# Emptying masked score products by chunk in a chunked linear-attention stage

## The chip, the cores and the metric

One core of a Trainium2 chip runs the whole program. The metric is the device time of one execution in microseconds (us). The engines have a queue each and run side by side: TensorE (PE, matmuls; PEld is its weight loads), VectorE (DVE), ScalarE (ACT), GpSimd (POOL) and SyncE (SP, which issues most transfers). A matmul writes into one of eight banks of PSUM (128 partitions x 2 KB), and DVE or ACT must empty a bank before it is written again.

## The reference

One layer of a hybrid block over 2048 tokens of width 1024, in float32. A combined projection feeds a band attention, an RWKV-7 time mixing and two gates; the two results are projected, gated, added and normalised, and a squared-relu MLP follows. The change is in the time mixing:

```python
def step(state, inp):
    r_t, w_t, k_t, v_t, aa_t, bb_t = inp
    sa = jnp.einsum('bhij,bhj->bhi', state, aa_t)
    state = (state * w_t[:, :, None, :] + sa[..., None] * bb_t[:, :, None, :]
             + v_t[..., None] * k_t[:, :, None, :])
    y = jnp.einsum('bhij,bhj->bhi', state, r_t)
    return state, y
xs = tuple(jnp.moveaxis(t, 1, 0) for t in (r_h, w_h, k_h, v_h, -kk, kk * a_h))
_, ys = lax.scan(step, init, xs)
```

## The kernel before

The tokens are worked in four groups of 512 (`G`). For each group the program runs `phase_rwkv`, then attention, then the merge; the MLP follows in two halves. Matrix products in float32 are made of three products of high and low parts; the dense products (`psd`, L92 and L131, 24 matmuls of 128x512 for each 128 columns) read weights that ACT casts to the high part (`whi`, L81) and DVE splits into the low part (`wlo`, L83), both in two buffers.

The time mixing turns the scan over tokens into products over chunks of 64 tokens (`C`), 8 chunks a group (`NC`). Its 8 heads are worked in four pairs (`p` 0 to 3): one head in partitions 0 to 63, the other (`par`=1) in 64 to 127. For a pair, `rwkv_pre` makes r, k, v and the decay, and from these A (the scaled -kk), r (scaled) and the keys B and K. `AR` holds A and r, `BK` holds B and K. The scores `ps_A` are, for each chunk and head, one product of BK with AR (64 rows, 128x128): B and K against A and r of the same chunk. They fill one bank for four chunks of one head, so a pair has four banks in two halves (`h`) of two. They come from the pool `pa`, which has two banks and serves nearly everything in this stage; the pool `pr` has two more (`wus`), for the chunk chain `ps_st` and, later, `ps_yt`.

From the scores DVE takes, bank by bank: the part that the inverse needs, scaled by the reciprocal norm `n2` (`NA`, L596, two operations of 32 partitions); A's own scores under a strict mask (`mS`) into the other half of AR (L602); r's scores under an inclusive mask, times the norm, into `BR` (L603). POOL has multiplied mask and norm ahead of that (`mN`, L500). `rwkv_inverse` then inverts the 32x32 diagonal blocks of two pairs at once on DVE: a stream transpose of NA into N, 31 steps (T, X), and transposes back (X1, XD). `rwkv_blocks` joins the blocks by two rounds of small products (`ps_t`), and `rwkv_trans` turns A (`ps_at`, L680), makes `ps_w`, `ps_ug`, `ps_tq`, `ps_s` and `ps_y`, and `recurrence` walks the eight chunks: `ps_st` on TensorE, then ST on DVE (L743), chunk after chunk.

The instructions of all engines are put in order by a scheduler with its own estimate of times. A few TensorE instructions are held back behind a numbered dense matmul of the group (`place`): the first score of p=0 behind number 150 (`SCORES`), ps_t behind 412 and 424, and 640 and 653 (`BLOCKS`), A's turning in p=0 behind 438 (`TURNED`). `k` of p=3 and others are scaled out of a dense bank by ACT at L401, and `lora_g` is a cast of ACT (L81).

Of the kernel before, what the change touches and what calls it, by code (L numbers as in the profile page):

```python
# [18 lines left out]
P = 128  # L19
# [37 lines left out]
class Block:  # L57
# [100 lines left out]
    def constants(self, ctx, mixing):  # L158
# [36 lines left out]
        self.mS = cp.tile([P, C], F32, name="mS")  # L195
        self.mI = cp.tile([P, C], F32, name="mI")
        for t, op in ((self.mS, ALU.is_gt), (self.mI, ALU.is_ge)):
# [247 lines left out]
    def rwkv_pre(self, g, p, rp, NA, between=lambda: None):  # L445
# [52 lines left out]
        mN = self.tp.tile([P, 2, NC, C], F32, tag="mN", bufs=1, name="mN")  # L498
        for par in range(2):
            nc.gpsimd.tensor_tensor(  # L500
                mN[:, par],
                self.mI[:, None, :].to_broadcast((P, NC, C)),
                n2[:, :, par, None].to_broadcast((P, NC, C)),
                ALU.mult,
            )
        between()

        AR = rp.tile([P, NC, 3, C], F32, tag="AR", name="AR")
# [3 lines left out]
        for par in range(2):  # L512
            rw = slice(par * C, par * C + C)
            nc.vector.scalar_tensor_tensor(
                AR[rw, :, par], k3[rw], self.nkk[rw, col], E[rw, :, 0:C], op0=ALU.mult, op1=ALU.mult
            )
        nc.vector.tensor_tensor(AR[:, :, 2], r3, E[:, :, 1 : C + 1], ALU.mult)
# [42 lines left out]
        BR = rp.tile([P, NC, 2, 2, C], F32, tag="BR", name="BR")  # L560
# [15 lines left out]
        mS = self.mS[:, None, :].to_broadcast((P, 4, C))  # L576
        for h in range(2):
            cs = slice(h * 4, h * 4 + 4)

            both = [self.pa.tile([P, 4, P], F32, tag="a", name="ps_A") for _ in range(2)]  # L580
            for j in range(4):
                c = h * 4 + j
                for par, psA in enumerate(both):
                    rw = slice(par * C, par * C + C)
                    mm = nc.tensor.matmul(
                        psA[:, j].rearrange("p (s t) -> p s t", t=C),
                        BK[rw, c].rearrange("p s t -> p (s t)"),
                        AR[rw, c, par : 3 : 2 - par], start=True, stop=True,
                    )
                    if p == c == par == 0:  # L590
                        self.place(mm, SCORES)
            for par, psA in enumerate(both):
                ow = slice(C - par * C, P - par * C)
                for lo, w in ((0, C), (32, 32)):
                    hw = slice(par * C + lo, par * C + lo + 32)
                    nc.vector.tensor_tensor(  # L596
                        NA[hw, q, cs, 0:w],
                        psA[hw, :, lo : lo + w],
                        n2[hw, cs, par, None].to_broadcast((32, 4, w)),
                        ALU.mult,  # L600
                    )
                nc.vector.tensor_tensor(AR[ow, cs, par], psA[ow, :, 0:C], mS[ow], ALU.mult)  # L602
                nc.vector.tensor_tensor(BR[:, cs, par, 1], psA[:, :, C:P], mN[:, par, cs], ALU.mult)  # L603
# [3 lines left out]
    def rwkv_inverse(self, NA, rp):  # L607
# [4 lines left out]
            N, NA.rearrange("p q c t -> p t (q c)")[:, 0:32, None, :].to_broadcast((P, 32, 2, 2 * NC))  # L612
# [16 lines left out]
        X1 = ip.tile([P, 2, NC, 32], F32, tag="X1", name="X1")  # L629
# [12 lines left out]
    def rwkv_blocks(self, NA, Rs, b):  # L642

        nc, X1, XT = self.nc, self.X1, self.XT
        first, second = [], []
        Z = self.ip.tile([P, 2, NC, 32], F32, tag="Z", name="Z")
        parts = [(slice(r, r + 32), slice(r + 32, r + C)) for r in (0, C)]
        ps = self.pa.tile([P, 2, NC, 32], F32, tag="a", name="ps_t1")
        for q in range(2):
            for c in range(NC):  # L650
                for lo, hi in parts:
                    mm = nc.tensor.matmul(ps[hi, q, c], NA[lo, q, c, 32:64], X1[lo, q, c], start=True, stop=True)
                    first.append(mm)
        for lo, hi in parts:
            nc.scalar.copy(Z[hi], ps[hi])
        ps = self.pa.tile([P, 2, NC, 32], F32, tag="a", name="ps_t2")
        for q in range(2):
            for c in range(NC):
                for lo, hi in parts:
                    mm = nc.tensor.matmul(ps[lo, q, c], Z[hi, q, c], XT[hi, q, c, 32:64], start=True, stop=True)  # L660
                    second.append(mm)
        for mm, n in zip((first[0], second[0]), BLOCKS[b]):
            self.place(mm, n)
        for lo, hi in parts:
            nc.scalar.copy(XT[lo, :, :, 32:64], ps[lo])
        for q in range(2):
            Rs[q]["XT"] = XT[:, q]

    def rwkv_trans(self, p, R):
# [7 lines left out]
        for h, cs in enumerate(halves):  # L677
            ps = self.pa.tile([P, 4, P], F32, tag="a", name="ps_at")
            for j in range(4):
                mm = nc.tensor.transpose(ps[:, j], AR[:, h * 4 + j, 0:2].rearrange("p s t -> p (s t)"), self.ident)  # L680
                if p == 0 and h == 1 and j == 0:
                    self.place(mm, TURNED)
            for par in range(2):
                nc.scalar.copy(WA[rows[par], cs, 0], ps[rows[par], :, par * C : par * C + C])
        ps = self.pa.tile([P, NC, C], F32, tag="a", name="ps_w")
        for c in range(NC):
            for par in range(2):
                ow = rows[1 - par]
                nc.tensor.matmul(ps[rows[par], c], AR[ow, c, par], SV[ow, c, par], start=True, stop=True)
# [15 lines left out]
        for h, cs in enumerate(halves):  # L705
            ps = self.pa.tile([P, 4, 2, C], F32, tag="a", name="ps_tq")
            for j in range(4):
                c = h * 4 + j
                for par in range(2):
                    nc.tensor.matmul(  # L710
                        ps[rows[par], j], GT[rows[par], c], BR[rows[par], c, par], start=True, stop=True
                    )
# [3 lines left out]
            nc.vector.tensor_tensor(TQ[:, cs, 1], ps[:, :, 1], AR[:, cs, 2], ALU.add)  # L716
# [76 lines left out]
    def phase_rwkv(self, g, quads):  # L793
        tc = self.tc
        with ExitStack() as ctx:
# [13 lines left out]
            def pairs():  # L809
                return self.ip.tile([P, 2, NC, C], F32, tag="NA", name="NA")  # L810
# [20 lines left out]
            def rec_of(NA, Rs, b):  # L831
                self.rwkv_blocks(NA, Rs, b)
# [22 lines left out]
            rec = rec_of(NA, Rs, 0)  # L855
# [17 lines left out]
            for i in range(3):  # L873
                advance(inv, 8)
                gate()
                if i == 0:
                    b = rp.tile([P, 4, G], F32, tag="BR", name="cmb")
                    load([b[:, i] for i in range(4)])
                elif i == 1:
                    b, c = (rp.tile([P, n, G], F32, tag=t, name="cmb") for t, n in (("AR", 3), ("SV", 2)))  # L880
                    load([b[:, 0], b[:, 1], b[:, 2], c[:, 0]])
# [4 lines left out]
            rec = rec_of(NA, nxt, 1)  # L886
# [763 lines left out]
```

## Time and profile before

| | |
|---|---|
| median of 3 runs | 3199.93 us (3196.32 to 3201.05) |
| the profiled execution | 3198.07 us, span 3196.4 us |
| TensorE | 3147.3 us busy (98%) |
| DVE / ACT / POOL | 2235.8 / 1578.7 / 613.8 us busy |
| granted TensorE clock | 0.999 |

In the order of time each row has its start, its length, the engine and line, what it writes and reads, and the number of instructions that were merged; a bracket has the idle time ahead of it and who ended it. A matmul's length runs past the start of the next, so its price is the distance from start to start. A float32 matmul that is not a transpose leaves two records, so a score product of four chunks reads x8. In a list of waits each row has the total, how often, and the longest. Line numbers are those of the kernel before.

### The profile page before, as it was taken

Reading aid. Unit: us, or ns where it says so; the run is one execution under the profiler, and the core shown is the slowest. Engines: PE = TensorE matmul, PEld = TensorE weight load, DVE = VectorE, ACT = ScalarE, POOL = GpSimd, SP = SyncE. Lnnn points to the kernel's source line nnn. Section 1 sums busy time; section 2 is a strip of 40 time slices with the busy share of each in tenths; the row PEclk is TensorE's granted clock in tenths of the full one; section 3 lists DMA queues with packets and bytes.
Section 4 is the critical chain, followed back from the end, with each engine's and each line's share of the span. In section 5 each row is a group of like instructions: output and inputs, shape, how many; then the busy total and the mean of one; then the engine's idle time right before and its main releaser. Section 6 shows DMA issues by size and latency. Waiting matters only on the chain. (4 is left out here: it accounts for less than half of the span.)

```text
span 3196.4 us, 49803 instructions
## 1 busy us (share of the span) xinstructions
PE 3147.3 (98%) x18800; PEld 2575.3 (81%) x18800; DVE 2235.8 (70%) x3668; ACT 1578.7 (49%) x2511; POOL 613.8 (19%) x1119
## 2 busy tenths in 40 slices
PE   8999999999999999999999999999999999999998
PEld 6877788778888877888877888888888878888887
DVE  6785667776767786767876776877656768765564
ACT  5435645445745445745534755454544454444343
POOL 3222012132112222112222101221211112210000
PEclk9999999999999999999999999999999999999999
DMA  6245473157573246574236466554877866547565
GB/s 192 86 135 189 134 259 129 60 172 244 175 260 129 77 141 245 186 235 160 94 116 228 160 208 261 192 179 162 293 268 251 281 225 213 170 156 244 191 221 174
DMA packets 197477, 598.82 MB, mean 187 GB/s; under 512 B 25570, under 2 KB 25708, under 8 KB 197236
## 3 DMA queue, kind: packets, MB, share of 16 engines
q1 hardware_dynamic: 139124, 415.24, 40.1%
q0 software_dynamic: 48896, 163.61, 13.6%
q10 hardware_dynamic: 9216, 16.78, 1.4%
q8 instruction: 148, 2.42, 0.3%
q14 instruction: 93, 0.76, 0.1%
HBM read 431.67 MB, written 167.01 MB: 187 GB/s over the span
## 5 line engine op out<-in xcount | busy, mean ns | idle before, releaser
L1469 PE MATMUL ps_dn<-fop 128*128 128x512 f32 x2688 | 610.8, 389 | 0.0
L1469 PEld LDWEIGHTS ps_dn<-fop 128*128 128x128 f32 x2688 | 504.1, 188 | 104.7 <-DVE fop L83 0.2
L81 ACT CAST whi<-wraw 128x1024 fp32r<-128x1024 f32 x232 | 243.5, 1049 | 284.4 <-PE psd L92 202.5
L83 DVE TENSOR_TENSOR wlo<-wraw,whi 128x1024 fp32r<-128x1024 f32 x230 | 280.6, 1220 | 125.4 <-ACT whi L81 80.2
L92 PE MATMUL psd<-hh,whi 128*128 128x512 f32 x1328 | 357.9, 398 | 1.1 <-ACT k L401 1.0
L92 PE MATMUL psd<-hh,wlo 128*128 128x512 f32 x1328 | 356.8, 398 | 0.0
L92 PE MATMUL psd<-hl,whi 128*128 128x512 f32 x1328 | 354.3, 397 | 0.0
L92 PEld LDWEIGHTS psd<-hl,whi 128*128 128x128 f32 x1328 | 243.6, 188 | 47.9
L92 PEld LDWEIGHTS psd<-hh,wlo 128*128 128x128 f32 x1328 | 242.7, 188 | 48.3
L92 PEld LDWEIGHTS psd<-hh,whi 128*128 128x128 f32 x1328 | 241.2, 188 | 50.0 <-ACT k L401 1.6
L83 DVE TENSOR_TENSOR fop<-xraw,fop 128x1024 fp32r<-128x1024 f32 x112 | 137.0, 1223 | 176.2 <-ACT fop L81 175.8
L81 ACT CAST fop<-xraw 128x1024 fp32r<-128x1024 f32 x112 | 117.8, 1052 | 251.0 <-PE ps_dn L1469 191.9
L1339 POOL DMA_DIRECT2D xd<-X x192 | 104.1, 542 | 380.3 <-ACT X L1336 318.2
L83 DVE TENSOR_TENSOR fop<-wdraw,fop 128x1024 fp32r<-128x1024 f32 x112 | 136.6, 1219 | 19.7 <-ACT fop L81 19.4
L81 ACT CAST fop<-wdraw 128x1024 fp32r<-128x1024 f32 x112 | 117.6, 1050 | 35.7 <-DMA wdraw<-in_w_down_dram 22.7
L994 DVE CUSTOM_DVE_ANT_0 sc<-bias,ps_s 128x640 f32<-128x640 f32 (+4 forms) x128 | 93.8, 733 | 39.3 <-PE ps_s L988 23.3
L1012 DVE TENSOR_TENSOR PTl<-ps_pt,PTh 128x640 fp32r<-128x640 f32 (+4 forms) x128 | 94.3, 737 | 27.7 <-ACT PTh L1011 26.8
L1001 ACT ACTIVATE sc<-sc,mn 128x640 f32<-128x640 f32 (+4 forms) x128 | 97.8, 764 | 31.8 <-DVE mn L994 30.4
L81 ACT CAST s12h<-s 128x1024 fp32r<-128x1024 f32 x32 | 33.7, 1053 | 155.5 <-PE ps_u L92 155.5
L92 PE MATMUL ps_p<-yh,whi 128*128 128x512 f32 x256 | 101.7, 400 | 4.9 <-DVE th L1149 2.2
L92 PE MATMUL ps_p<-yl,whi 128*128 128x512 f32 x256 | 101.5, 397 | 0.3 <-DVE yl L83 0.2
L1178 PE MATMUL ps_o<-whi,mh 128*128 128x512 f32 x256 | 100.5, 392 | 0.7 <-DVE o L1189 0.6
(374 smaller groups left out, 6804.0 us busy)
## 6 DMA issues: line engine op xcount, KB each, us to landing
wraw<-in_w_in_dram SPq DMA_DIRECT2D x168, 512.0 KB, 3.7
xraw<-xd SPq DMA_DIRECT2D x112, 512.0 KB, 4.5
xd<-X POOLq DMA_DIRECT2D x192, 256.0 KB, 4.7
wraw<-in_w_up_dram SPq DMA_DIRECT2D x80, 512.0 KB, 4.4
wdraw<-wd SPq DMA_DIRECT2D x64, 512.0 KB, 4.8
wdraw<-in_w_down_dram SPq DMA_DIRECT2D x48, 512.0 KB, 5.0
gd<-gate ACTq DMA_DIRECT2D x64, 256.0 KB, 2.5
wd<-cmb POOLq DMA_DIRECT2D x64, 256.0 KB, 3.7
```

The costliest lines, as they stand in the source:

```text
L81: high = self.high = self.nc.scalar.copy(hi, src)
L83: self.low = lower.tensor_tensor(lo, src, hi.bitcast(F32), ALU.subtract).ins
L92: mm.append(nc.tensor.matmul(ps, l, r, start=n == 0, stop=n == last).ins)
L994: least = nc.vector.tensor_tensor_reduce(sc[:, 0:n], bias[:, s0:640], pss[:, c0 : c0 + n], 1.0, 3.0e38, ALU.add, ALU.min, mn,)
L1001: nc.scalar.activation(sc[:, 0:n], sc[:, 0:n], AF.Exp, scale=-1.0, bias=mn, accum_out=sm[:, col : col + 1])
L1012: nc.vector.tensor_tensor(lv, pst[:, 0:nk], hv.bitcast(F32), ALU.subtract)
L1178: nc.tensor.matmul(ps[t], l[:, k, ts], r[:, k % 2], start=k == 0 and j == 0, stop=k == KB - 1 and j == 2)
L1339: nc.gpsimd.dma_start(self.xd[q][i // 2][:, i % 2], src)
L1469: nc.tensor.matmul(ps, o[:, l, k, sl], o[:, r, k], start=start and n == 0, stop=stop and n == end)
```

## The change

- The two masks become one tile, inclusive and strict side by side, and POOL's product of mask and norm goes.
- `AR` has A and r in two planes. A is written by one DVE operation for both heads.
- Every chunk and head of the scores is emptied by one DVE operation (128 x 128: score times norm times mask) into BR, which has a third plane for A's scores; ACT copies from there the part that the inverse needs, 32 partitions at a time.
- `ps_t` and `ps_w` read BR's third plane. NA has half the width.
- `ps_at` turns A of two chunks in one transpose, so four transposes of one tile serve a pair instead of eight of two; four ACT copies take them to WA.
- In the first two pairs the second half of the scores uses the two banks of `pr`.
- The tiles that later hold loads for the MLP (`cmb`) are cut out of BR and AR differently.

```diff
-        mN = self.tp.tile([P, 2, NC, C], F32, tag="mN", bufs=1, name="mN")
-        for par in range(2):
-            nc.gpsimd.tensor_tensor(
-                mN[:, par],
-                self.mI[:, None, :].to_broadcast((P, NC, C)),
-                n2[:, :, par, None].to_broadcast((P, NC, C)),
-                ALU.mult,
-            )
...
-        AR = rp.tile([P, NC, 3, C], F32, tag="AR", name="AR")
+        AR = rp.tile([P, 2, NC, C], F32, tag="AR", name="AR")
...
-        for par in range(2):
-            rw = slice(par * C, par * C + C)
-            nc.vector.scalar_tensor_tensor(
-                AR[rw, :, par], k3[rw], self.nkk[rw, col], E[rw, :, 0:C], op0=ALU.mult, op1=ALU.mult
-            )
-        nc.vector.tensor_tensor(AR[:, :, 2], r3, E[:, :, 1 : C + 1], ALU.mult)
+        nc.vector.scalar_tensor_tensor(AR[:, 1], k3, self.nkk[:, col], E[:, :, 0:C], op0=ALU.mult, op1=ALU.mult)
+        nc.vector.tensor_tensor(AR[:, 0], r3, E[:, :, 1 : C + 1], ALU.mult)
...
-        BR = rp.tile([P, NC, 2, 2, C], F32, tag="BR", name="BR")
+        BR = rp.tile([P, NC, 2, 3, C], F32, tag="BR", name="BR")
...
-            both = [self.pa.tile([P, 4, P], F32, tag="a", name="ps_A") for _ in range(2)]
+            pool, tag = (self.pr, "wus") if p < 2 and h else (self.pa, "a")
+            both = [pool.tile([P, 4, P], F32, tag=tag, name="ps_A") for _ in range(2)]
...
             for par, psA in enumerate(both):
-                ow = slice(C - par * C, P - par * C)
-                for lo, w in ((0, C), (32, 32)):
-                    hw = slice(par * C + lo, par * C + lo + 32)
-                    nc.vector.tensor_tensor(
-                        NA[hw, q, cs, 0:w],
-                        psA[hw, :, lo : lo + w],
-                        n2[hw, cs, par, None].to_broadcast((32, 4, w)),
-                        ALU.mult,
-                    )
-                nc.vector.tensor_tensor(AR[ow, cs, par], psA[ow, :, 0:C], mS[ow], ALU.mult)
-                nc.vector.tensor_tensor(BR[:, cs, par, 1], psA[:, :, C:P], mN[:, par, cs], ALU.mult)
+                for j in range(4):
+                    c = h * 4 + j
+                    nc.vector.scalar_tensor_tensor(
+                        BR[:, c, par, 1:3].rearrange("p s t -> p (s t)"), psA[:, j], n2[:, c, par : par + 1], masks,
+                        op0=ALU.mult, op1=ALU.mult,
+                    )
+                for i in range(2):
+                    hw = slice(par * C + 32 * i, par * C + 32 * i + 32)
+                    cs = slice(h * 4, h * 4 + 4)
+                    nc.scalar.copy(NA[hw, q, cs], BR[hw, cs, par, 2, 32 * i : 32 * i + 32])
...
-        for h, cs in enumerate(halves):
-            ps = self.pa.tile([P, 4, P], F32, tag="a", name="ps_at")
-            for j in range(4):
-                mm = nc.tensor.transpose(ps[:, j], AR[:, h * 4 + j, 0:2].rearrange("p s t -> p (s t)"), self.ident)
-                if p == 0 and h == 1 and j == 0:
-                    self.place(mm, TURNED)
-            for par in range(2):
-                nc.scalar.copy(WA[rows[par], cs, 0], ps[rows[par], :, par * C : par * C + C])
+        ps = self.pa.tile([P, 4, P], F32, tag="a", name="ps_at")
+        for j in range(4):
+            mm = nc.tensor.transpose(ps[:, j], AR[:, 1, 2 * j : 2 * j + 2].rearrange("p c t -> p (c t)"), self.ident)
+            if p == j == 0:
+                self.place(mm, TURNED)
+        for par in range(2):
+            for h in range(2):
+                nc.scalar.copy(WA[rows[par], h:NC:2, 0], ps[rows[h], :, par * C : par * C + C])
```

With this the scheduler orders the stage anew; the order of the attention, the merge, the MLP and of SP's transfers stays. The names in the rows below are those of the words above; x8 of ps_A is eight products of which both heads alternate, unless said otherwise, x4 is four of one head.

TensorE in the first pair, before:

```order
L92 MATMUL psd<-hh,whi 128x512 x7
L585 MATMUL ps_A<-AR,BK 128x128 x8
L92 MATMUL psd<-hh,whi 128x512
L92 MATMUL psd<-hl,whi 128x512 x6
L585 MATMUL ps_A<-AR,BK 128x128 x4
L92 MATMUL psd<-hl,whi 128x512 x2
L585 MATMUL ps_A<-AR,BK 128x128 x4
L92 MATMUL psd<-hh,wlo 128x512 x8
```

And now, from the same dense matmul on:

```order
L571 MATMUL ps_A<-AR,BK 128x128 x8
L92 MATMUL psd<-hh,whi 128x512 x7
L571 MATMUL ps_A<-AR,BK 128x128 x8
L92 MATMUL psd<-hh,whi 128x512
L92 MATMUL psd<-hl,whi 128x512 x8
L92 MATMUL psd<-hh,wlo 128x512 x8
```

The half that uses the pool `pr` has moved ahead of seven dense matmuls, and the two runs of four have become one of eight.

TensorE in the second pair, before, from the turning of BK (`ps_bk`) on:

```order
L565 MATMUL ps_bk<-ident,BK 128x128 x4
L92 MATMUL psd<-hh,wlo 128x512
L585 MATMUL ps_A<-AR,BK 128x128 x4
L92 MATMUL psd<-hh,wlo 128x512 x2
L585 MATMUL ps_A<-AR,BK 128x128 x4
L92 MATMUL psd<-hh,whi 128x512 x2
L585 MATMUL ps_A<-AR,BK 128x128 x4
L92 MATMUL psd<-hh,whi 128x512 x2
L585 MATMUL ps_A<-AR,BK 128x128 x4
L92 MATMUL psd<-hh,whi 128x512 x4
```

And now, from the dense matmuls that stand ahead of ps_bonus on:

```order
L92 MATMUL psd<-hh,wlo 128x512 x5
L571 MATMUL ps_A<-AR,BK 128x128 x4
L92 MATMUL psd<-hh,wlo 128x512 x2
L571 MATMUL ps_A<-AR,BK 128x128 x4
L92 MATMUL psd<-hh,wlo 128x512
...
L552 MATMUL ps_bk<-ident,BK 128x128 x4
L92 MATMUL psd<-hh,wlo 128x512
L571 MATMUL ps_A<-AR,BK 128x128 x8
L92 MATMUL psd<-hh,wlo 128x512 x2
```

Half of the scores now stands 20 dense matmuls earlier, and the other half is a run of eight: three of one head, three of the other, one and one.

TensorE in the last pair, among the chunk chain, before:

```order
L585 MATMUL ps_A<-AR,BK 128x128 x8
L738 MATMUL ps_st<-ST,TQ 64x64 x2
L742 MATMUL ps_y<-ST,TQ 64x64 x2
L738 MATMUL ps_st<-ST,TQ 64x64 x2
L742 MATMUL ps_y<-ST,TQ 64x64 x2
L92 MATMUL psd<-hh,wlo 128x512 x2
L92 MATMUL psd<-hh,whi 128x512 x2
L585 MATMUL ps_A<-AR,BK 128x128 x4
L92 MATMUL psd<-hh,whi 128x512 x3
L585 MATMUL ps_A<-AR,BK 128x128 x4
```

And now:

```order
L571 MATMUL ps_A<-AR,BK 128x128 x4
L723 MATMUL ps_st<-ST,TQ 64x64 x2
L727 MATMUL ps_y<-ST,TQ 64x64
L571 MATMUL ps_A<-AR,BK 128x128 x4
L727 MATMUL ps_y<-ST,TQ 64x64
L723 MATMUL ps_st<-ST,TQ 64x64 x2
L727 MATMUL ps_y<-ST,TQ 64x64 x2
L92 MATMUL psd<-hh,wlo 128x512
L571 MATMUL ps_A<-AR,BK 128x128 x4
L92 MATMUL psd<-hh,wlo 128x512
L571 MATMUL ps_A<-AR,BK 128x128 x4
L723 MATMUL ps_st<-ST,TQ 64x64 x2
```

The eight (three, three, one, one) are two fours with a step of the chunk chain between them, and two single dense matmuls separate the others.

More of the change, by code (lines that the diff above doesn't have):

```diff
@@ L193, in constants @@
         )
-        self.mS = cp.tile([P, C], F32, name="mS")
-        self.mI = cp.tile([P, C], F32, name="mI")
-        for t, op in ((self.mS, ALU.is_gt), (self.mI, ALU.is_ge)):
+        self.masks = cp.tile([P, 2, C], F32, name="masks")
+        for t, op in ((self.masks[:, 1], ALU.is_gt), (self.masks[:, 0], ALU.is_ge)):
             nc.vector.memset(t, 1.0)
@@ L585, in rwkv_pre @@
                     mm = nc.tensor.matmul(
-                        psA[:, j].rearrange("p (s t) -> p s t", t=C),
-                        BK[rw, c].rearrange("p s t -> p (s t)"),
-                        AR[rw, c, par : 3 : 2 - par], start=True, stop=True,
+                        psA[:, j].rearrange("p (s t) -> p s t", t=C), BK[rw, c].rearrange("p s t -> p (s t)"),
+                        AR[rw, :, c], start=True, stop=True,
                     )
@@ L628, in rwkv_inverse @@
             yield
-        X1 = ip.tile([P, 2, NC, 32], F32, tag="X1", name="X1")
+        X1 = ip.tile([P, 2, NC, 32], F32, tag="NA", name="X1")
         nc.vector.transpose(X1.rearrange("p q c (j d) -> p j d (q c)", d=2), X.rearrange("p r j -> p j r"))
@@ L640, in rwkv_inverse, with rwkv_blocks @@
         self.X1, self.XT = X1, XT
-    def rwkv_blocks(self, NA, Rs, b):
+    def rwkv_blocks(self, Rs, b):
         nc, X1, XT = self.nc, self.X1, self.XT
@@ L650, in rwkv_blocks @@
             for c in range(NC):
-                for lo, hi in parts:
-                    mm = nc.tensor.matmul(ps[hi, q, c], NA[lo, q, c, 32:64], X1[lo, q, c], start=True, stop=True)
+                for par, (lo, hi) in enumerate(parts):
+                    off = Rs[q]["BR"][lo, c, par, 2, 32:64]
+                    mm = nc.tensor.matmul(ps[hi, q, c], off, X1[lo, q, c], start=True, stop=True)
                     first.append(mm)
@@ L688, in rwkv_trans @@
                 ow = rows[1 - par]
-                nc.tensor.matmul(ps[rows[par], c], AR[ow, c, par], SV[ow, c, par], start=True, stop=True)
+                nc.tensor.matmul(ps[rows[par], c], BR[ow, c, par, 2], SV[ow, c, par], start=True, stop=True)
         nc.scalar.copy(WA[:, :, 1], ps)
@@ L710, in rwkv_trans @@
                     nc.tensor.matmul(
-                        ps[rows[par], j], GT[rows[par], c], BR[rows[par], c, par], start=True, stop=True
+                        ps[rows[par], j], GT[rows[par], c], BR[rows[par], c, par, 0:2], start=True, stop=True
                     )
@@ L809, in pairs @@
             def pairs():
-                return self.ip.tile([P, 2, NC, C], F32, tag="NA", name="NA")
+                return self.ip.tile([P, 2, NC, 32], F32, tag="NA", name="NA")
             gates = iter(range(2 * KB))
@@ L829, in places, with rec_of @@
                 return between
-            def rec_of(NA, Rs, b):
-                self.rwkv_blocks(NA, Rs, b)
+            def rec_of(Rs, b):
+                self.rwkv_blocks(Rs, b)
                 yield
@@ L854, in phase_rwkv @@
             gate()
-            rec = rec_of(NA, Rs, 0)
+            rec = rec_of(Rs, 0)
             NA = pairs()
@@ L876, in phase_rwkv @@
                 if i == 0:
-                    b = rp.tile([P, 4, G], F32, tag="BR", name="cmb")
+                    b = rp.tile([P, 6, G], F32, tag="BR", name="cmb")
                     load([b[:, i] for i in range(4)])
                 elif i == 1:
-                    b, c = (rp.tile([P, n, G], F32, tag=t, name="cmb") for t, n in (("AR", 3), ("SV", 2)))
-                    load([b[:, 0], b[:, 1], b[:, 2], c[:, 0]])
+                    c = rp.tile([P, 2, G], F32, tag="AR", name="cmb")
+                    load([b[:, 4], b[:, 5], c[:, 0], c[:, 1]])
             advance(inv)
@@ L885, in phase_rwkv @@
             gate()
-            rec = rec_of(NA, nxt, 1)
+            rec = rec_of(nxt, 1)
             load([self.tmp("cmb") for _ in range(4)])
```

7 lines of the change are left out of this document (3 added, 4 removed).

## Prediction

> **What bounds the kernel now.** I read the head of the page first, then the list of TensorE's waits, then the order of time on TensorE in one group's recurrent stage, last the DVE, ACT and POOL work beside it.
>
> ```profile
> span 3196.4 us, 49803 instructions
> ...
> PE 3147.3 (98%) x18800; PEld 2575.3 (81%) x18800; DVE 2235.8 (70%) x3668; ACT 1578.7 (49%) x2511; POOL 613.8 (19%) x1119
> ```
> ```profile
> PE ps_r L366 <- POOL each L365: 11.1, 3, 9.5
> PE ps_st L738 <- DVE ST L743: 4.2, 4, 1.1
> ...
> PE psd L92 <- ACT k L401: 1.0, 4, 0.3
> ```
> TensorE is busy for 98% of the span. Its longest wait is the start (11.1 us); of the stage that the change touches, the list names 4.2 us behind ST and 1.0 us behind k, a quarter of it in each of four groups. So time is won almost only by taking work out of TensorE's queue, or by keeping that queue from changing form; relief on DVE or POOL counts where one of those waits hangs on it. The profiled execution took 3198.07 us (span 3196.4), 1.9 us under the median 3199.93 of the runs, inside their spread.
>
> The price of a dense matmul, and a wait that the list puts down to nothing:
>
> ```profile
> 128.38 1.98 PE L92 MATMUL psd<-hh,wlo 128*128 128x512 f32 x8
> 130.19 1.29 PE L92 MATMUL psd<-hh,whi 128*128 128x512 f32 x5
> 131.55 1.20 PE L652 MATMUL ps_t<-X,NA 32*32 32x32 f32 x64
> ```
> ```profile
> 130.34 1.15 DVE L630 STREAM_TRANSPOSE X<-X 128x512 f32<-128x512 f32 x1
> ```
> Eight dense matmuls take 1.81 us from start to start, 0.226 each. Five then take 1.36, 0.23 more than 1.13: the inverse's X1 is finished at 131.49, just as ps_t starts. About 0.1 us of that is a wait; the first inverse has no slack at all.
>
> **The change, part by part.** *The scores of a group's first pair (p=0).*
>
> ```profile
> 55.58 1.75 PE L92 MATMUL psd<-hh,whi 128*128 128x512 f32 x7
> 57.26 1.16 PE L585 MATMUL ps_A<-AR,BK 64*128 64x128 f32 x16
> 58.35 0.50 PE L92 MATMUL psd<-hh,whi 128*128 128x512 f32 x1
> 58.69 1.55 PE L92 MATMUL psd<-hl,whi 128*128 128x512 f32 x6
> 60.20 1.13 PE L585 MATMUL ps_A<-AR,BK 64*128 64x128 f32 x8
> 61.26 0.73 PE L92 MATMUL psd<-hl,whi 128*128 128x512 f32 x2
> 61.92 1.16 PE L585 MATMUL ps_A<-AR,BK 64*128 64x128 f32 x8
> 63.00 2.12 PE L92 MATMUL psd<-hh,wlo 128*128 128x512 f32 x8
> 64.96 0.40 PE L428 MATMUL ps_z<-lora,whw 128*128 128x512 f32 x1
> ```
> Each score product is two records. Eight products that alternate between the two heads' partitions and banks (x16) take 1.09 us; four of one head (x8) take 1.06 to 1.08. So four in one half of the array cost as much as eight in both. From 55.58 to 64.96 are 9.38 us, with 24 dense matmuls (5.43), so 3.95 are scores and changes of form. After, the order has eight, seven dense, eight: 2 x 1.09, the island of dense between them (1.85 for 7, so 0.27 over), 0.09 into the first and 0.15 out of the last, 2.69. Saved: 1.26 us. It asks that both pairs of banks are free and that BK and AR are there; ps_bk has read BK before.
>
> The Trainium skill, "TensorEngine Tiling (Array Packing)", section Key Properties, says that different tiles "can execute LdWeights and Matmul in parallel", and that a change of tiling mode drains TensorE. The rows above bear out both; were the tiles not parallel, this edit would save only the one island, some 0.3 us, and the whole sum would be near -10 us.
>
> *The second pair (p=1).*
>
> ```profile
> 90.96 1.16 PE L585 MATMUL ps_A<-AR,BK 64*128 64x128 f32 x8
> 92.04 0.73 PE L92 MATMUL psd<-hh,wlo 128*128 128x512 f32 x2
> 92.71 1.16 PE L585 MATMUL ps_A<-AR,BK 64*128 64x128 f32 x8
> ...
> 97.28 1.20 PE L92 MATMUL psd<-hh,whi 128*128 128x512 f32 x4
> ```
> ```profile
> 193.48 1.49 PE L585 MATMUL ps_A<-AR,BK 64*128 64x128 f32 x16
> 194.90 0.33 PE L738 MATMUL ps_st<-ST,TQ 64*64 64x64 f32 x4
> ```
> Four times four with two dense between each: 6.32 us less 6 x 0.226, 4.96. After, two fours stand earlier (1.08 + 0.67 + 1.07 less two dense, and 0.2 for entry and exit: 2.6), and eight in the order three, three, one, one, which took 1.42 us at 193.48, plus 0.1: 4.1 in all. Saved: 0.9 us.
>
> *The last two pairs* keep two banks. p=2 has the same number of fours and islands: nothing. In p=3 the order splits the eight of 193.48 into two fours among the ps_st products (2 x 1.05 for 1.42, +0.7) and has about two islands more (2 x 0.22): +1.1 us. Against that stands this wait:
>
> ```profile
> 188.75 0.33 PE L738 MATMUL ps_st<-ST,TQ 64*64 64x64 f32 x4 [1.06 <-DVE ST L743]
> ```
> ST stands on DVE behind AR and BK of p=3, and there DVE loses the rest of what follows. I take the 1.06 as gone, so p=3 is zero; its bounds are +1.1 (the wait stays) and -0.4 (it goes, and the second four overlaps).
>
> *DVE, POOL and ACT per pair.*
>
> ```profile
> L743 DVE SCALAR_TENSOR_TENSOR ST<-ps_st,gC,S 128x64 f32<-128x64 f32 x112 | 27.4, 277 | 4.4 <-PE ps_st L738 4.4
> L602 DVE TENSOR_TENSOR AR<-ps_A,mS 64x256 f32<-64x256 f32 x64 | 27.0, 422 | 1.1
> L596 DVE TENSOR_TENSOR NA<-ps_A,n 32x256 f32<-32x256 f32 x64 | 26.6, 416 | 16.0 <-PE ps_A L585 14.9
> L603 DVE TENSOR_TENSOR BR<-ps_A,mN 128x256 f32<-128x256 f32 x64 | 26.6, 415 | 0.7
> L514 DVE SCALAR_TENSOR_TENSOR AR<-k,nkk,E 64x512 f32<-64x512 f32 x32 | 23.9, 746 | 0.6
> L596 DVE TENSOR_TENSOR NA<-ps_A,n 32x128 f32<-32x128 f32 x64 | 18.6, 290 | 0.9
> ```
> ```profile
> 84.06 1.54 DVE L530 TENSOR_TENSOR BK<-tk,Ei 64x512 f32<-64x512 f32 x1
> ```
> ```profile
> 83.52 3.00 POOL L500 TENSOR_TENSOR mN<-mI,n 128x512 f32<-128x512 f32 x2
> ```
> ```profile
> L684 ACT COPY WA<-ps_at 64x256 f32<-64x256 f32 x64 | 23.5, 367 | 39.6 <-PE ps_at L680 38.4
> ```
> DVE now spends 4 x (422 + 416 + 415 + 290) ns = 6.2 us on a pair's scores. The sixteen new operations, 128 wide with a scalar by partition, lie between the same form at 64 wide (277) and 256 wide (422); near the first I take 0.31, 5.0 us, bounds 4.4 and 6.8. One AR operation of 746 goes as well. BK at 84.06 took 1.54 us with POOL's mN beside it, and there is no mN any more. So DVE is ahead by about 2 us a pair, more where mN fell on BK. Of that only the waits above are on the path: 0.1 at ps_t (the inverse starts earlier), and the 1.06.
>
> The Trainium skill, "VectorE: DVE Perf Modes", section on the TRN2 errata, speaks against cutting one wide operation into small ones: each pays its fixed cost, and it advises 512 elements or more. By its row for PSUM sources (120 cycles and one per element at 0.96 GHz) an estimate for 128 elements is 0.26 us, 4.1 us for sixteen; the sum stays, since the fours were narrow already.
>
> ACT gets eight copies of 32x128 a pair, under the 367 ns of 64x256; I take 0.28, 2.2 us. ACT is at 49%, so they hide, except where the queue is in order before something awaited: six stand before lora_g and two before k's scaling in p=2, where TensorE already waits (1.0 us in all). Priced: nothing (z runs earlier too) to +0.6 a group; the weights' casts behind other copies have their buffers more than a dense group (5.4 us) ahead. What the inverse needs now goes through DVE and then ACT. Where its first operation stands now:
>
> ```profile
> 98.83 2.02 DVE L611 STREAM_TRANSPOSE N<-NA 128x1024 f32<-128x1024 f32 x1
> ```
> In p=1 half of the sixteen operations are done before ps_bonus, and the last eight products end at about 90.96 - 1.26 + 2.6 + 1.42 = 93.7, where the last four ended at 97.2. DVE's last eight take 2.5 us from the first filled bank on, ACT's last copies 0.6 behind them, and a split of weights that ran after the transpose now runs before it: N starts near 97.5 with that split out of the way, some 2.5 us of DVE time ahead, AR's 0.75 comes to it, and TensorE comes 2.2 earlier. The inverse is not later.
>
> *Turning A.*
>
> ```profile
> L680 PE MATMUL ps_at<-ident,AR x128: 270/273/330, 136.9 to 1700.9; 128*128 128x128 f32 x128
> ```
> ```profile
> 136.89 0.66 PE L680 MATMUL ps_at<-ident,AR 128*128 128x128 f32 x4
> 137.30 1.86 PE L92 MATMUL psd<-hh,wlo 128*128 128x512 f32 x7
> ...
> 152.26 0.60 PE L680 MATMUL ps_at<-ident,AR 128*128 128x128 f32 x4
> 152.83 1.15 PE L689 MATMUL ps_w<-SV,AR 64*64 64x64 f32 x32
> ```
> 128 become 64: four fewer in each of 16 pairs. Four cost 0.41 us ahead of dense work, 0.57 ahead of ps_w. With two of each a group: 2.0 us. The four copies to WA now all follow one tile: 4 x 0.367 = 1.5 us, then the copy of ps_w, ahead of ps_ug; ps_w and the dense matmuls cover most of it; I put 0.3 a group against it. Net -1.7.
>
> **Sum, a group:** -1.26 - 0.9 + 0 - 1.7 - 0.1 = -4.0 us; four groups: -16 us. 3198.07 - 16 = 3182, 3199.93 - 16 = 3184; I say 3183.
>
> **The rivals.** *Only the transposes pay*: the scores' gathering is lost again, because TensorE waits for BK in p=1, for the slower release in p=2, or the 1.06 stays. For it: all three hang on one DVE queue. Then four fewer transposes at 0.41, 16 times: -6.6 us, 3192. *DVE turns into the bound of the chunk chain*, the slower case: if the 128-wide operation takes not 0.31 but 0.6 us, sixteen are 9.6 us for 6.2; the ST behind them is 3.4 us late in p=2 and again in p=3, where ps_st has waited already, and the first inverse by about 1; 8 a group against the 4 won, so 3198 + 16 = 3214. It decides from about 0.5 us on (32 operations each 0.12 over today's 0.39 eat the 4 us), and 422 ns for twice the width speaks against it. *Nothing moves*: ACT's copies ahead of k and of the inverse cost 2.2 us a group, the p=3 islands 1.1 with the wait still there: -4.0 + 3.3 = -0.7 a group, 3195.
>
> **How the numbers follow.** Forecast 72%, transposes alone 14%, nothing 8%, slower 6%. This kernel's measurement tells about 0.2% (6.4 us) from no change: 3193.5 is the border. The transposes-alone case lies around it, two thirds inside the gain: faster 0.80, same 0.14, slower 0.06. Range 3175 to 3195: below, p=3 at its -0.4, the 0.3 ahead of ps_ug not needed and k's quarter microsecond gone are 1 us a group, 3179, with the spread of the runs (3 to 4 us) under it; above, the transposes alone with the same spread.
>
> **What would show it.** ps_at x64 instead of x128; ps_A as x16 twice in p=0 with 1.1 us each; the sixteen operations at 0.25 to 0.4; no wait of ps_st for ST near 1 us; ps_t without a wait; k's wait not above 0.9 a group; the stages of attention and after it as long as before. It is wrong if ps_A shows gaps behind DVE, if ps_t waits for X1, or if p=3 grows by more than a microsecond.

## The result, and the profile after

| | median, us | lowest to highest | profiled execution's span |
|---|---|---|---|
| before | 3199.54 | 3194.96 to 3201.64 | 3196.4 |
| changed | 3180.74 | 3177.98 to 3182.83 | 3180.2 |

The changed kernel takes 0.9944 of the time of the kernel before (95% interval 0.9934 to 0.9954), 18.8 us less; 3183 was forecast, from 3175 to 3195.

The head of the page of the changed kernel, its list of TensorE's waits, and three groups of instructions:

```profile
span 3180.2 us, 49723 instructions
...
PE 3135.3 (99%) x18736; PEld 2567.8 (81%) x18736; DVE 2190.1 (69%) x3652; ACT 1617.5 (51%) x2639; POOL 570.8 (18%) x1087
```
```profile
PE psd L92 <- ACT k L400: 3.4, 4, 0.8
...
PE ps_ug L684 <- ACT WA L675: 1.8, 4, 0.5
```
```profile
L580 DVE SCALAR_TENSOR_TENSOR BR<-ps_A,n,masks 128x128 f32<-128x128 f32 x256 | 70.5, 343 | 20.7 <-PE ps_A L571 20.7
L587 ACT COPY NA<-BR 32x128 f32<-32x128 f32 x128 | 37.9, 296 | 70.2 <-DVE BR L580 65.8 <-ACT gate L775 3.2
L669 ACT COPY WA<-ps_at 64x256 f32<-64x256 f32 x64 | 23.4, 366 | 37.6 <-PE ps_at L664 37.0
```

TensorE is busy 12 us less. Gone from the list are ps_st behind ST (4.2 before), ps_s behind TQ and the second ps_t behind Z, which stood in it with these rows of the kernel before:

```profile
PE ps_s L723 <- DVE TQ L716: 2.2, 4, 0.9
...
PE ps_t L660 <- ACT Z L655: 0.8, 4, 0.2
```

The wait of the dense products for k has grown, 3.4 us for 1.0, and ps_ug now waits for WA, 1.8 us, 0.45 a group.

The same instruction can be found in both traces, so the difference of its two start times tells how far the changed kernel is ahead there, and the growth of that difference from one place to the next is what the stretch between them gave. The places are the first ps_ss of each pair, the first ps_t after each inverse, and the first transposes of y (ps_yt). Between the first ps_yt of a group and its second ps_t the difference stays within 0.01 us. The mean of the four groups, in us a group; each group lies within 0.04 of it, but for the last stretch, which goes from -1.86 to -2.50:

| stretch | what lies in it | changed - before |
|---|---|---|
| p=0's ps_ss to p=1's | scores of p=0 | -1.29 |
| to ps_t | scores of p=1, first inverse | -0.87 |
| to p=2's ps_ss | ps_t, A of p=0 turned | -0.88 |
| to p=3's ps_ss | A of p=1 turned, scores of p=2, k | -0.44 |
| to ps_yt | scores of p=3 among the chunks | +1.15 |
| second ps_t to the second ps_yt | A of p=2 and p=3 turned, TQ | -2.11 |
| sum | | -4.43 |

Four groups give -17.7 us. The spans differ by 16.2; the rest is attention and MLP, which the change does not reorder and where two runs differ by such amounts (one wait of ps_u for x alone is 2.4 us here and 0.3 before).

The scheduler also moves products across these places. In the changed kernel two dense products and ten records of the chunk chain have changed sides at p=3's ps_ss; by their prices (0.45 us, and some 0.4 at the 0.61 that sixteen such records take) that cancels, and where a run moves more it is said there.

The timeline of TensorE after, for p=0 (start, length, instructions):

```profile
55.87 1.16 PE L571 MATMUL ps_A<-AR,BK 64*128 64x128 f32 x16
56.96 1.88 PE L92 MATMUL psd<-hh,whi 128*128 128x512 f32 x7
58.77 1.16 PE L571 MATMUL ps_A<-AR,BK 64*128 64x128 f32 x16
59.87 0.50 PE L92 MATMUL psd<-hh,whi 128*128 128x512 f32 x1
60.20 2.00 PE L92 MATMUL psd<-hl,whi 128*128 128x512 f32 x8
```

Two blocks of eight products, 1.09 and 1.10 us each, seven dense products between: what took 3.95 us is 2.68. The scores of p=3:

```profile
188.45 1.16 PE L571 MATMUL ps_A<-AR,BK 64*128 64x128 f32 x8
189.53 0.33 PE L723 MATMUL ps_st<-ST,TQ 64*64 64x64 f32 x4
189.70 0.28 PE L727 MATMUL ps_y<-ST,TQ 64*64 64x64 f32 x2
189.90 1.16 PE L571 MATMUL ps_A<-AR,BK 64*128 64x128 f32 x8
...
191.91 1.16 PE L571 MATMUL ps_A<-AR,BK 64*128 64x128 f32 x8
193.00 0.51 PE L92 MATMUL psd<-hh,wlo 128*128 128x512 f32 x1
193.43 1.16 PE L571 MATMUL ps_A<-AR,BK 64*128 64x128 f32 x8
```

Four blocks of four, 1.08 us each and each an island of its own, where the kernel before had its first eight in 1.42 us.

Last, DVE ahead of the TQ of p=2; the first two rows are of the kernel before, the other two of the changed one:

```profile
247.29 0.69 DVE L1231 TENSOR_TENSOR cmb<-cmb 128x512 f32<-128x512 f32 x1 [8.33 <-DMA cmb<-in_w_down_dram]
247.90 0.42 DVE L713 TENSOR_TENSOR TQ<-ps_tq,id 128x256 f32<-128x256 f32 x1
```
```profile
240.93 0.69 DVE L1216 TENSOR_TENSOR cmb<-cmb 128x512 f32<-128x512 f32 x1 [5.08 <-DMA cmb<-in_w_down_dram]
243.45 0.42 DVE L698 TENSOR_TENSOR TQ<-ps_tq,id 128x256 f32<-128x256 f32 x1 [1.83 <-PE ps_tq L695]
```

Before, TQ stood on DVE behind a sum whose load came late, and TensorE waited for TQ. POOL issues this load, behind the transfer of the y stage that follows the second inverse: at 239.86 before and at 234.04 after. So the load comes 6.4 us earlier, and TQ waits for TensorE.

### The profile page after: what moved, and what is told of

It is laid out like the page before. It is cut to its first block, busy times and chain, and to the rows that moved or that the text cites. A ratio compares the mean times of both kernels' runs of the same rounds, so it can differ in the third digit from the quotient of the medians.

```text
span 3180.2 us, 49723 instructions
## 1 busy us (share of the span) xinstructions
PE 3135.3 (99%) x18736; PEld 2567.8 (81%) x18736; DVE 2190.1 (69%) x3652; ACT 1617.5 (51%) x2639; POOL 570.8 (18%) x1087
## 4 chain that ended last, share of the span: by engine, by line
PE 60%; issue 10%; POOL 2%; DMA 2%; ACT 2%; DVE 1%; SPq 0%; POOLq 0%; DVEq 0%; ACTq 0%
PE ps_dn L1454 19%; PE psd L92 16%; PE ps_u L92 9%; PE ps_o L1163 3%; PE ps_p L92 2%; PE ps_pv L1003 2%; POOL xd L1324 2%; PE ps_s L973 1%; PE ps_pt L992 1%; PE ps_A L571 1%; PE ps_tq L695 0%; DMA x<-in_x_dram 0%; PE ps_ht L1202 0%; PE ps_ug L684 0%; PE ps_st L723 0%
## 5 line engine op out<-in xcount | busy, mean ns | idle before, releaser
L83 DVE TENSOR_TENSOR fop<-wdraw,fop 128x1024 fp32r<-128x1024 f32 x112 | 136.6, 1220 | 19.0 <-ACT fop L81 18.8
```

The costliest lines, as they stand in the source:

```text
L83: self.low = lower.tensor_tensor(lo, src, hi.bitcast(F32), ALU.subtract).ins
```

## The experiments

All are edits of the changed kernel, and the times are medians. Their stretches, in us a group against the kernel before:

| kernel | p=0 | p=1 | to p=2 | to p=3 | p=3 | second turning | sum | time |
|---|---|---|---|---|---|---|---|---|
| changed | -1.29 | -0.87 | -0.88 | -0.44 | +1.15 | -2.11 | -4.4 | 3180.74 |
| two_banks | +0.02 | -0.20 | -0.52 | -0.41 | +1.16 | -2.09 | -2.0 | 3188.48 |
| eight_turns | -1.30 | -0.86 | -0.60 | +0.07 | +1.17 | -1.12 | -2.6 | 3188.11 |
| mask_alone | +0.01 | -0.20 | -0.22 | +0.06 | +1.15 | -1.18 | -0.4 | 3198.67 |
| late_inverse | -1.28 | -0.83 | -0.87 | -0.42 | +2.61 | -1.42 | -2.2 | 3188.87 |
| gathered | -1.29 | -2.15 | -0.87 | +0.27 | -2.05 | -1.60 | -7.7 | 3165.64 |
| gathered3 | -1.29 | -0.87 | -0.89 | -0.43 | -1.01 | -2.01 | -6.5 | 3170.19 |
| gathered_two_banks | -1.27 | +2.32 | +0.92 | -0.43 | +1.15 | -2.11 | +0.6 | 3195.81 |
| pool_na | -1.28 | -0.87 | -0.80 | -1.11 | -0.58 | -1.47 | -6.1 | 3172.24 |
| gathered_pool_13 | -1.28 | -2.15 | -0.74 | -1.11 | -1.34 | -0.62 | -7.2 | 3167.52 |
| gathered_pool_123 | -1.30 | -2.17 | -0.79 | -0.41 | -0.92 | -1.33 | -6.9 | 3168.77 |

**Two banks for all scores.**

```
-            pool, tag = (self.pr, "wus") if p < 2 and h else (self.pa, "a")
+            pool, tag = self.pa, "a"
```

> All score tiles go back to the pool of two banks; the masked operation and the turning of two chunks at once stay. Theory (the two extra banks are what lets eight products stand together): p=0 gives back 1.3 us a group and p=1 0.8, the later stages keep their gain, so some 8 us more than the changed kernel, about 3189 (3187 to 3192). Rival (the stage is set by DVE's inverse and the chain of chunks, TensorE's earlier scores are waited away later): within 2 us of the changed kernel, 3179 to 3183.

3188.48, ratio to the kernel before 0.9967 (0.9954 to 0.998): 7.7 us come back, as the theory said. p=0 loses all of its gain (1.31), p=1 0.67 of its 0.87; another 0.36 goes before p=2, of it 0.2 because ps_ug waits for WA eight times (2.6 us) instead of four (1.8). N starts at 99.79 instead of 97.20.

**One chunk of A turned at a time.**

```
-        for j in range(4):
-            mm = nc.tensor.transpose(ps[:, j], AR[:, 1, 2 * j : 2 * j + 2].rearrange("p c t -> p (c t)"), self.ident)
+        for h, cs in enumerate(halves):
+            ps = self.pa.tile([P, 4, P], F32, tag="a", name="ps_at")
+            for j in range(4):
+                c = h * 4 + j
+                mm = nc.tensor.transpose(ps[:, j], AR[:, 1, c - h : c - h + 2].rearrange("p c t -> p (c t)"), self.ident)
...
```

> A of one chunk is turned at a time again: eight transposes and two bank tiles a pair instead of four and one, everything else as changed. Theory (transposes are paid on TensorE one by one, and the wait of ps_s for TQ has another cause): 1.7 to 2.0 us a group come back, 0.9 of it before p=2's ps_ss and 0.4 to 0.9 after the second inverse, no wait of ps_s for TQ: about 3188 (3186 to 3190). Rival (the wait of ps_s for TQ went because a pair uses one bank tile less, so that the banks fall otherwise): that wait of about 0.55 us a group comes back as well, about 3190, and the list of waits shows it again.

3188.11, ratio 0.9968 (0.9955 to 0.998), 7.4 us. The three stretches with a turning in them lose 0.28, 0.51 and 0.99, 1.8 us a group. The list of waits holds no wait of ps_s for TQ, so the bank rival falls: that wait does not hang on the number of bank tiles.

**The masked operation alone** (both edits above together).

> Two banks for all scores and eight transposes a pair again: of the change only the masked operation (with its layout, the copies on ACT and the missing mN) is left. If the three parts add up, the time is that of the changed kernel and 7.7 and 7.4 us more, 3196 (3193 to 3198): a gain of about 3 us over the kernel before, made of the waits of ps_s for TQ and of ps_t that are gone, less the longer wait for k and the longer p=3. If the parts need each other (the early inverse hides only behind earlier scores): 3199 or more.

3198.67, ratio 0.9995 (0.9986 to 1.0005), between the two expectations. By the stretches the parts do add up: -4.43 + 2.39 + 1.79 is -0.3, measured -0.4. By the medians they would give 3195.9, 2.8 us less than measured, which is within the spread of its runs (3194.64 to 3201.94). The masked operation with its layout is worth nothing in time by itself. It pays 0.6 us a group for k and 1.15 in p=3 (the wait for ST that goes is within it). Against that the waits for TQ and Z go, 0.76, and the stretch that held the wait for X1 is 0.20 shorter. Some 1.2 us a group of what it gains stand in no list of waits and were not traced. What it brings is the layout in which two chunks are turned at once.

**A later second inverse.**

```
+        for _ in range(times):
-        nc.vector.transpose(
+            nc.vector.transpose(
...
-            inv = self.rwkv_inverse(NA, rp)
+            inv = self.rwkv_inverse(NA, rp, 3)
```

> The transpose that starts the second inverse of each group is done three times instead of once (the same result), which puts 4.2 us of DVE work ahead of that inverse and changes nothing else. Theory (DVE's queue: the second inverse is 4.75 us earlier after the change; with it go the y stage behind it, its transfer and the load that the sum ahead of TQ on DVE waits for): ps_t still does not wait, but ps_s waits for TQ again, 0.5 to 2 us a group, so 3183 to 3188. Rival (that wait went with the bank tiles or with the regrouped loads of the sums): no such wait, 3181 within 2. Second rival (the inverse had no slack left): ps_t waits for X1 by a microsecond or more a group.

3188.87, ratio 0.9969 (0.996 to 0.9979). The list of TensorE's waits:

```profile
PE psd L92 <- DVE wlo L83: 4.5, 4, 1.1
...
PE ps_s L709 <- DVE TQ L702: 2.1, 2, 1.1
```

And the sum ahead of the TQ of p=2 on DVE:

```profile
244.42 0.69 DVE L1217 TENSOR_TENSOR cmb<-cmb 128x512 f32<-128x512 f32 x1 [7.32 <-DMA cmb<-in_w_down_dram]
```

The load is issued 3.4 us later than in the changed kernel (237.44), and the wait for TQ is back, 1.1 us each in two groups out of four. So it does hang on the time of the second inverse, by way of this load and DVE's queue. It is smaller than it might be, because TensorE is late there too, by a wait that no theory named: a dense product waits 1.1 us a group for the lower half of its weights, whose subtraction stands behind the inverse on DVE. With it the stretch of p=3 is 1.46 us longer, the larger part of what this run lost.

**All eight products of a block together.** `queue_behind` keeps the first instruction behind the second in TensorE's queue.

```
-                for par, psA in enumerate(both):
+                for par in (1, 0) if p > 0 else (0, 1):
+                    psA = both[par]
...
+                    if p > 0:
+                        if j == 0 and par == 1:
+                            lead = mm.ins
+                        else:
+                            self.queue_behind(mm.ins, lead)
```

> In p=1 to p=3 the first product of a block starts with the second head, and the other seven are queued behind it, so that all eight products of a block stand together in every block. Theory (four of one head cost as much as eight that alternate, and p=3 grew because its blocks fell apart among the ps_st products): a block costs 1.1 us plus 0.3 for coming and going, which saves about 1.1 us a group in p=1, 1.5 in p=2 and 2.2 in p=3; 4.5 a group, about 3163 (3159 to 3168). Rival (a block then waits for the later of its two banks, 1.4 us of DVE work, and the chain of chunks and the inverse behind it become late): what is saved is waited away, 3178 to 3185.

3165.64, ratio 0.9898 (0.9883 to 0.9913): 33 us less than the kernel before, 15 less than the changed one, and the fastest kernel of this study. The blocks of p=3, and the two longest of the waits that it adds:

```profile
187.24 1.49 PE L572 MATMUL ps_A<-AR,BK 64*128 64x128 f32 x16
...
190.73 1.71 PE L572 MATMUL ps_A<-AR,BK 64*128 64x128 f32 x16
```
```profile
PE ps_z L427 <- DVE BR L587: 3.3, 4, 0.8
...
PE ps_st L730 <- DVE ST L735: 1.8, 4, 0.4
```

p=1 gains 1.28 more and p=3 3.20, and p=2 loses 0.71. Of these 3.20 and 0.71 some 0.6 is only a shift: one dense product and ten records of the chunk chain that the changed kernel has behind p=3's ps_ss stand ahead of it here. In p=2 the scores do take 1.07 us less, and the waits of ps_z for the emptying of a bank (0.8) and of ps_st for ST (0.4) take most of that back, while the wait for k falls to 0.4. The time lies in the expected range, but the parts were otherwise (1.5 was expected in p=2).

The second turning loses 0.5, since ps_s waits for TQ again, 1.4 us in two groups. The load was issued at 231.60, 2.4 us earlier than in the changed kernel, but took 8.8 us to land for 6.8, while TensorE had come 3.7 us further ahead. So the gain at TQ is not safe: pool_na and gathered_pool_13, which also bring TensorE forward, wait there too.

**The same in p=3 alone.** The edit is the last one with p == 3 for p > 0, but a block starts with the first head, and its first product also stands behind the operation that empties the later bank.

> As the gathered kernel, but in p=3 alone, and there each block is also put behind the operation that empties the later of its banks; p=0 to p=2 as changed. Theory (p=3 cost 1.15 us a group more than before because its blocks of eight fell into fours): from p=3's ps_ss to the next stage about 3 us a group come back, 12 in all, so 3169 (3166 to 3173). Rival (in the gathered kernel p=3 gained because p=1 and p=2 came earlier): under 1.5 us a group, 3175 to 3181.

3170.19, ratio 0.9903 (0.9887 to 0.992). p=3 goes from +1.15 to -1.01, 2.16 us, with p=0 to p=2 as in the changed kernel: so the order with fours costs p=3 2.16 us against blocks of eight, and the rival, that p=3 gained because p=1 and p=2 came earlier, falls. The scores themselves take 2.74 us for 4.34; the rest goes with the changes of form. TensorE's rows of p=3 go from one form to another (`128*128`, `64*64`, `64*128`) 14 times in the kernel before, 22 times in the changed one, 17 times here and 12 times in the gathered kernel. Of the other microsecond that the gathered kernel gains in p=3, 0.6 is the shift named there.

**Two banks, but the order forced in p=0 and p=1.** Two banks as above, and the edit before this one with p < 2 for p == 3.

> Two banks for all scores again, but in p=0 and p=1 the order is forced: a block of eight products waits until both banks are empty and then stands together. Theory (it is the order, eight that alternate, that pays; the two extra banks only let the planner find it): p=0 keeps its 1.3 us a group and p=1 gains what it gained in the gathered kernel, so 3176 (3173 to 3182). Rival (the extra banks are needed, since a block now waits for 2.7 us of emptying and the inverse starts later): ps_t waits for X1 and p=1 loses its gain, 3184 to 3190.

3195.81, ratio 0.9996 (0.9987 to 1.0006). The timeline in p=0, and the wait that sets p=1:

```profile
57.53 1.16 PE L572 MATMUL ps_A<-AR,BK 64*128 64x128 f32 x16
...
61.12 1.17 PE L572 MATMUL ps_A<-AR,BK 64*128 64x128 f32 x16
```
```profile
PE ps_t L645 <- DVE X L622: 14.1, 4, 3.5
```

Both are right, in different pairs. p=0 keeps its whole gain (-1.27) with two banks: on TensorE it is the order that pays. In p=1 the last scores come later, N starts at 99.16 for 97.20, and DVE's order then has some 3.5 us of p=2's operations ahead of the transpose that ends the inverse; ps_t waits 3.5 us a group for it. The stretch also has four dense products (0.91) from the next one. The gathered kernel's -2.15, 0.91 and 3.52 make +2.28, measured +2.32: the order gains here too, and the wait takes it.

The next stretch is 1.80 us longer than in the changed kernel, though it has those four products less, so 2.71 are lost there. Here is its start in the first group, and the window from 132 to 140 (its length, TensorE's busy time and instructions, the granted clock, DMA's share and GB/s):

```profile
132.82 1.92 PE L645 MATMUL ps_t<-X,BR 32*32 32x32 f32 x64 [3.52 <-DVE X L622]
134.67 3.35 PE L92 MATMUL psd<-hl,whi 128*128 128x512 f32 x7
```
```profile
132.00:140.00 8.00, 7.18 (x92) 0.57 0.23 68
```

The same ps_t took 1.20 us in the kernel before, and seven dense products 1.75. Around the end of this wait the granted clock is 0.5, for 6.83 us in three groups and 3.41 in one; in the kernels before and after it is 1.00 through the whole stage. Half of these spans, less what lies in the wait itself, is 2.7 us a group in the mean: the whole loss. So 3.5 us of waiting cost 6.2, and that is why the time lies above the rival's range. Whether two banks would do with another order on DVE wasn't tried.

**The copies to NA on POOL.**

```
-                    nc.scalar.copy(NA[hw, q, cs], BR[hw, cs, par, 2, 32 * i : 32 * i + 32])
+                    nc.gpsimd.tensor_copy(NA[hw, q, cs], BR[hw, cs, par, 2, 32 * i : 32 * i + 32])
```

> The eight copies a pair that bring A's scores into NA are done by POOL instead of ACT. Theory (TensorE's wait for k grew from 1.0 to 3.4 us because six such copies stand before k's scaling on ACT): that wait falls back to about 1 us, 0.6 a group, and nothing else moves: 3178 (3176 to 3181). Rival (POOL is slower at such copies, so that the inverse starts later and TQ waits again): the 2.4 us are given back, 3180 to 3184.

3172.24, ratio 0.9913 (0.9898 to 0.9928): 8.5 us less than the changed kernel, where 2.7 were expected. The wait for k is gone altogether, and the stretch to p=3 gains 0.67, so these copies on ACT were its cause. The surprise is p=3, 1.73 us: with ACT's copies moved, the order there came out with its first eight products together again, which takes 0.75 from the scores, and with 17 changes of form for 22.

```profile
187.77 1.49 PE L571 MATMUL ps_A<-AR,BK 64*128 64x128 f32 x16
190.93 1.16 PE L571 MATMUL ps_A<-AR,BK 64*128 64x128 f32 x8
192.44 1.16 PE L571 MATMUL ps_A<-AR,BK 64*128 64x128 f32 x8
```

The rival is half right as well: TQ waits 1.9 us in three groups.

**Each masked operation twice.**

```
-                for j in range(4):
+                for j in (0, 0, 1, 1, 2, 2, 3, 3):
```

> Each of the sixteen masked operations of a pair is issued twice (the second writes the same values), 16 x 0.343 = 5.5 us more DVE work a pair: a test of the case in which DVE becomes the bound. By the prediction's rival (an operation at 0.5 us is where the gain is eaten; here it takes 0.69 in effect): 6 to 11 us a group over the changed kernel, 3205 to 3225, with waits of TensorE for ST, BR or X1. If DVE has slack enough to hide it: under 3190.

3247.22, ratio 1.0149 (1.0134 to 1.0164), 66 us over the changed kernel and above the 3225 that the expectation ended with.

```profile
PE psd L92 <- DVE wlo L83: 11.2, 4, 2.8
...
PE ps_t L637 <- DVE X L614: 10.9, 7, 2.5
PE psd L92 <- ACT r L400: 7.8, 4, 2.8
PE ps_A L571 <- DVE BR L580: 6.6, 4, 1.7
```

The recurrent stage becomes 17.6 us a group longer. The row for DVE in p=0 of the changed kernel tells what was added:

```profile
57.18 2.15 DVE L580 SCALAR_TENSOR_TENSOR BR<-ps_A,n,masks 128x128 f32<-128x128 f32 x8
```

Eight operations take 2.15 us; less the length of the last (0.34), seven steps of 0.26. A row's mean of 343 ns is the length of one, of which 0.08 overlaps with the next. Sixteen more a pair are 4.2 us, 16.6 a group. That TensorE loses 17.6 does not mean that all of it was on the path. TensorE waits 11.7 us a group in this stage for 1.5 in the changed kernel, 10.2 more, so some 6 us of the added work stay hidden. The rest of the loss, 7.4, goes with the clock: around these waits the granted clock is 0.5 for 17 to 24 us a group, where the changed kernel has 1.00, and half of that outside the waits is 9.7 us in the mean, enough to cover it. Without it the 10.2 would be some 41 us, within the 6 to 11 a group that were expected.

**The gathered order and the copies on POOL.** Both edits; p in (1, 3), and p > 0.

> The gathered order in p=1 and p=3, where it paid, and the copies to NA on POOL. If the gains add up (1.3 us in p=1, 0.7 in p=2 by the wait for k, 3.2 in p=3 a group, less some 2 us in all for TQ, which waits again): 3162 (3159 to 3166). If POOL's later copies and the gathered p=3 stand in each other's way: 3167 to 3172.

> The same with p=2 gathered as well. There the gathered kernel lost 0.7 us a group against the changed one, 0.8 of it the wait of ps_z for the block's emptying; with ACT free of the copies the wait for k is not behind it: 3164 (3160 to 3168), 1 to 3 us more than with p=2 left alone.

3167.52, ratio 0.9905 (0.9891 to 0.992), and 3168.77, ratio 0.9909 (0.9893 to 0.9926). Neither adds to the gathered kernel. The first lies in its second expectation, the other just above its range. Against the changed kernel the first gains 1.28 in p=1 and 0.67 in p=2, as expected, and 2.49 of the expected 3.2 in p=3; the second turning loses 1.5, where ps_s waits for TQ (2.5 us in three groups) and ps_t for Z (1.4). Against the gathered kernel its p=3 is 0.7 worse (-1.34 for -2.05), but some 0.5 of that is a shift: the gathered kernel has one dense product more and twenty records of the chunk chain less behind p=3's ps_ss than this one. In the second, ps_z waits 0.83 us a group again, and the wait for k is back (2.7 us).

## Why the prediction was right, and where it was not

The time and the sum were right (-4.0 a group forecast, -4.43 measured). The mechanism of the parts that bring the gain, p=0, p=1 and the turning, was right too; that the rest came out near zero was luck, since errors cancelled there.

- *p=0*: -1.26 forecast, -1.29 measured; undone in two_banks, kept in gathered_two_banks. The mechanism is shown: eight that alternate cost what four of one head cost (1.09 and 1.06 to 1.08 us).
- *p=1 and ps_t*: -0.9 and -0.1 forecast, -0.87 measured, of it 0.67 for the banks and 0.2 without them. N was put at 97.5 and starts at 97.20.
- *Turning A*: -1.7 forecast; undoing it costs 1.8. The 0.3 that was put against it for the copies to WA shows as the new wait of ps_ug, 0.45.
- *The masked operation*: 0.31 was put for one, between 0.277 and 0.422 (the second is not the same form, as the prediction says, but a product of two tensors, L602); its length is 0.343, and its step 0.26. The prediction added up lengths, here and for the work that it replaced, and so saw 5.0 us for 6.2; the row of p=0 above says 4.3 us (twice 2.15) now, and before it was 6.2, from the start of the first of these rows to the end of the last:

```profile
58.45 0.71 DVE L596 TENSOR_TENSOR NA<-ps_A,n 32x256 f32<-32x256 f32 x2 [1.39 <-PE ps_A L585]
...
64.22 0.41 DVE L603 TENSOR_TENSOR BR<-ps_A,mN 128x256 f32<-128x256 f32 x1
```

  The estimate from the Trainium skill, "VectorE: DVE Perf Modes", section on the TRN2 errata, was 0.26 us for each and 4.1 for sixteen: the trace agrees with it as a step from start to start, not as the length that a profile shows. The rule there that speaks against small operations did not decide here.
- *p=2, k*: nothing to +0.6 a group was allowed for ACT's copies ahead of k; it came at the upper end (3.4 us in all for 1.0), and pool_na shows that these copies make it.
- *p=3*: zero was forecast, +1.15 measured. By the prediction's own sign ("It is wrong if [...] p=3 grows by more than a microsecond") this part was wrong. The wait for ST did go, as said, and the scores went from 3.59 to 4.34 us, the +0.7 that was put. The mis-sized term is the islands: 0.44 was put for two, and the order makes eight more changes of form (22 for 14), since products of the chunk chain too stand alone among dense ones, at 183.45 and 184.14 for example. What is left of +1.15 without the scores' 0.75 and with the 1.06 of the wait added is some 1.4 us. The bound of +1.1 was set for the case in which the wait stays; it was reached although the wait went.
- *TQ*: the step "Of that only the waits above are on the path: 0.1 at ps_t (the inverse starts earlier), and the 1.06." failed. The waits of ps_s for TQ, 2.2 us, and of the second ps_t for Z, 0.8, stood in the list of the kernel before and were passed over. The first was DVE waiting for a transfer, and an earlier inverse sends that transfer off earlier.
- *The rival in which DVE becomes the bound*: it did not come, but it was nearer than said. The prediction counted 32 operations a group as exposed, from about 0.5 us on; with 0.26 more for each of the 64, TensorE waited 10.2 us longer, what some 39 of them take, and lost 7.4 more, which the lower clock around these waits can cover. late_inverse, with 4.2 us more a group in one place, lost half of them.

So +1.15 and +0.6 were missed on one side, and on the other the waits for TQ and Z (0.76) with the 1.2 or so of mask_alone that no list names. What made those stays open.

## What to carry to other kernels

Products that fill half of TensorE's rows pay only when a block alternates between the halves; look at how the order groups them, since the same products in fours cost twice as much, and a planner that goes by when each bank falls free will split them. Tie the block together by one dependency, and see that the engine that empties the banks keeps its lead. And go through every wait of the stage in the list of before: a small wait behind a transfer can hang on an engine that one thinks has slack, and two errors of a microsecond can hide in a sum that comes out right. When a run is slower than its waits explain, read the granted clock around them, too.

## What the hardware showed that was not expected

- Start to start, the masked operation of 128x128 from PSUM takes 0.26 us, while its recorded length is 0.343. Costs of back-to-back operations on DVE are to be read from the length of a run of them.
- Waits of TensorE can cost more than their length. In these traces the granted clock falls to 0.5 for spans of 3.41 to 13.65 us, each of which (but for the last of every kernel, at its end) begins between 1.2 us before and 3.9 us after the end of a TensorE wait of 1.4 us or more: 3.5 us in gathered_two_banks, 1.66 to 2.8 in stt_twice, and 2.35 (ps_u for x) in the changed kernel. Not every such wait has one: one of 2.80 us in stt_twice has none.
- POOL copies 32x128 as fast as ACT: two take 0.61 us on either, in the rows of the changed kernel and of pool_na:

```profile
58.33 0.61 ACT L587 COPY NA<-BR 32x128 f32<-32x128 f32 x2 [1.66 <-DVE BR L580]
```
```profile
57.60 0.61 POOL L587 COPY NA<-BR 32x128 f32<-32x128 f32 x2 [1.78 <-DVE BR L580]
```

  The mean is 363 ns on POOL against ACT's 296, but that comes from eight copies out of 128. Beside the masked operations of DVE, 62 copies took 284 ns in the mean. The eight that began beside a split of weights on DVE ended 0.15 us after it, or after the split that followed, and took 1.2 or 1.8 us, as here the first of two:

```profile
95.30 1.21 DVE L83 TENSOR_TENSOR wlo<-wraw,whi 128x1024 fp32r<-128x1024 f32 x1
```
```profile
95.44 1.55 POOL L587 COPY NA<-BR 32x128 f32<-32x128 f32 x2 [0.42 <-DVE BR L580]
```
